# A 192-byte pad ahead of the weight pools, and a larger `plain` count for the first gate-and-up block

## The chip, the cores and the metric

The kernel runs on one core of one Trainium2 chip. The metric is the device time of one execution in microseconds (us). The time before is the median of three runs, 1911.58 us (1909.17 to 1911.75). One further execution was taken with the hardware profiler; it took 1910.38 us, of which 1908.3 us lie between the first and the last instruction (its span).

## The reference

One decoder layer on 256 tokens of width 2048, all in float32. A combined projection feeds three token mixers and their merge gates; then come a SwiGLU feed-forward part and a gated embedding part:

```
h = rms_norm(x, g_mix);  z = h @ w_in            # 2048 x 17424
u_a = short_conv_mixer(...) @ w_sc_out;  u_b = conformer_conv_mixer(...) @ w_cf_out;  u_c = gla_mixer(...) @ w_gla_out
x = x + (sigmoid(m_a)*u_a + sigmoid(m_b)*u_b + sigmoid(m_c)*u_c) @ w_o
gate, up = split(rms_norm(x, g_ffn) @ w_gate_up)  # 2048 x 11264
x = x + (silu(gate) * up) @ w_down
x = x + (p @ w_ple) * sigmoid(rms_norm(x, g_ple) @ w_ple_gate)
return rms_norm(x, g_final)
```

## The kernel before, in words

Every large product is made of matmuls with 128 x 128 of the activations as the stationary operand and 128 x 512 of a weight matrix as the moving operand. A weight tile is loaded as a `raw` tile (128 partitions x 2 x 512 floats, 4096 bytes per partition), and split into two float32r parts: ScalarE writes `whi` (a rounding copy), VectorE writes `wlo = raw - whi`. Activations are split the same way, and each product is the sum of three matmuls: hi by hi, hi by lo, lo by hi. So each 128 x 512 piece of a weight costs six matmuls (three for each half of the 256 tokens), and TensorE (PE) reads its moving operand straight from the `whi` and `wlo` tiles.

The work has two phases, each with its own set of pools (`open_pools`, L481; opened at L489 and L1317). In a pool, a tile's buffers lie one behind the other along a partition, and the pools of a phase are stacked one behind the other.

- **First phase** (L489 to L1316, to about 1069 us of the profile): w_in, the three mixers' output matrices and w_o, in groups of 512 columns. `run` (L655) walks over chunks of four 128-row blocks: it issues the loads two chunks ahead (`issue`, L561, from SyncE's queue), the splits one chunk ahead (`split_w`, L584, which calls `split`, L514), and then the chunk's matmuls (`products`, L639; matmuls at L649 to L651). Its pools are `gla` (one buffer for each of ten tiles), `raws` (5 buffers), `wparts` (5 `whi` and 5 `wlo`), `t4` (5 tiles of 4096 bytes for intermediate results), in this order, and 5 + 3 banks of PSUM. Between the groups stand short batches of other PE work: transposes of results (`transpose_block`, L712), scores of the linear attention (L927, L954), its output (L997 to L999). The stationary operands of the big products (`hhi`, `hlo`, `ohi`, `mT` and others) are tiles of the pool `t8`, which lasts through both phases.
- **Second phase** (from L1317): w_gate_up, w_down, w_ple, w_ple_gate. A recording planner (`Flow`, L114) orders loads, splits, matmuls (`three`, L242; matmuls at L244 to L246) and results by estimated times. Its pools are `raws` (6), `sums` (1), `wparts` (7 and 7), `t4` (3), and 7 + 1 banks of PSUM; the first of them starts at the byte where the first phase's `gla` started.

The pools that last through both phases end at byte 130560 of a partition, which is 255 x 512. The tiles of the first phase's `gla` pool take 4 x 512 + 2048 + 1920 + 1024 + 4096 + 2048 + 1984 = 15168 bytes there (`siga0`, L551, is the last of them), which is 29 x 512 + 320. So `raws`, `wparts` and `t4` of the first phase, whose tiles are all 4096 bytes, begin 320 bytes past a multiple of 512, every buffer of them. In the second phase every such buffer begins at a multiple of 512.

The second phase's gate and up products go in eleven blocks (`Quad`, L63; `add_quad`, L254). A block has eight pairs of 128-row blocks; `PAIRS = "soosooso"` (L1259) gives each pair a kind. Pairs of kind `o` split two raw tiles. Where a pair stands early in its block, at a position below `plain`, both splits are of the usual form. Behind that, the `wlo` of one of the two tiles is made another way (`neg` in `split_ops`, L211 to L225): ScalarE writes `-whi` into it (L220) and a DMA from GpSimd's (POOL's) queue adds the weights from memory onto it (L221), an adding load. Pairs of kind `s` never have an adding load. The two lines that decide it:

```
            kind = g.pairs[p]
...
                               neg=None if pos < g.plain else g.w[:, 2 * p : 2 * p + 2, g.cs[1] : g.cs[1] + NB])
```

`pos` counts the places in `order`. The first block is given an order and a `plain` of its own by `START` (L1426); all other blocks have the order 0 to 7 and `plain` 0.

Of the kernel before, what the change touches and what calls it, by code (L numbers as in the profile page):

```python
# [10 lines left out]
F32 = mybir.dt.float32  # L11
# [8 lines left out]
P = 128  # L20
# [440 lines left out]
def kernel(  # L461
# [17 lines left out]
    pools = {}  # L479

    def open_pools(**sizes):  # L481
# [8 lines left out]
        gla=(1,), raws=(5,), wparts=(5,), t4=(5,), acc=(5, PSUM), misc=(3, PSUM)  # L490
# [58 lines left out]
    s10 = pools["gla"].tile([P, 4, P], F32, name="s10")  # L549
    junk = const.tile([P, NB], F32, name="junk")  # L550
    siga0 = pools["gla"].tile([P, 2, 248], F32, name="siga0")  # L551
    featT = {}

    x_v = x[0].rearrange("(h p) d -> p h d", p=P)
# [781 lines left out]
    def quad_end(j):  # L1336
        def f(g, ps, part):
            v = g.v
            if part == 0:
                g.s = med("gs")  # L1340
            m, s = g.m, g.s

            def sig(h):
                return flow.op("A", 0.7, lambda: act.activation(out=s[:, h, :], in_=m[:, h, :], func=AF.Sigmoid, scale=rr("f", h)))

            def rm(h):
                return flow.op("D", 0.65, lambda: stt(m[:, h, :], m[:, h, :], rr("f", h), s[:, h, :], ALU.mult, ALU.mult))

            def last(h):
                return flow.op("D", 0.65, lambda: stt(m[:, h, :], v[:, h, :], rr("f", h), m[:, h, :], ALU.mult, ALU.mult))  # L1350

            if part == 0:
                return [
                    flow.op("D", 0.7, lambda: tt(m[:, 0, :], m[:, 0, :], ps["2"], ALU.add)),
                    sig(0),
                    rm(0),
                ]
            if part == 1:
                return [
                    flow.op("D", 0.7, lambda: tt(m[:, 1, :], ps["4"], v[:, 1, :], ALU.subtract)),  # L1360
                    sig(1),
                    rm(1),
                ]
            if part == 2:
                return [
                    flow.op("D", 0.7, lambda: tt(v[:, 1, :], v[:, 1, :], ps["5"], ALU.add)),
                    flow.op("D", 0.7, lambda: tt(v[:, 0, :], v[:, 0, :], ps["5"], ALU.add)),
                    last(1),
                ]
            ops = [flow.op("D", 0.7, lambda: tt(v[:, 0, :], v[:, 0, :], ps["3"], ALU.add)), last(0)]  # L1370
            flow.transposes(ops[-1], [a_stat(j, m, z) for z in (0, 2)])
            return ops

        return f
# [13 lines left out]
    def x_part(c, j):  # L1388

        def pe_part(b):  # L1390
            four(b, xr[c], j)

        def rest(b):
            quad_stat(2 * c + j // 2, b, med("sz", (P, 8, P)))

        return pe_part, rest, 2.0, ("f", 2 * c + j // 2)
# [26 lines left out]
        return f  # L1423

    NJ = 11
    START = ((1, 2, 0, 3, 4, 5, 6, 7), 2)  # L1426
    flow.transposes(None, [x_part(3, j) for j in (0, 2)])
    plan = []
    for lo, hi in ((0, 3), (3, 6), (6, 9), (9, NJ)):
        for j in range(lo, hi):  # L1430
            plan.append(Quad(w_gu_v, j * NB, (NJ + j) * NB, PAIRS, quad_mid, quad_end(j), *(START if j == 0 else ())))
        for c in range(4):
# [148 lines left out]
```

## Time and profile before

| | |
|---|---|
| median of three runs | 1911.58 us (1911.75, 1909.17, 1911.58) |
| the profiled execution | 1910.38 us, span 1908.3 us |
| mean granted TensorE clock | 0.996 of full speed |
| busy: PE, VectorE (DVE), ScalarE (ACT), POOL | 98%, 69%, 55%, 4% of the span |
| matmuls | 8589 records |
| adding loads (POOL, L221) | 53 |

How to read it: an engine's busy time is the union of its instructions; matmuls overlap, and their ends are modelled, so the pace of PE is read from the starts of its matmuls. "Idle before" a group is the time its engine stood still just ahead of those instructions, with the engine or transfer that ended the wait. The view by form gives each group of like instructions with its count, busy time and mean duration; the timeline gives single instructions with their start and duration in us. L12 is line 12 of the kernel before; the changed kernel's lines from 552 on have numbers larger by one.

### The profile page before, as it was taken

To read this page: it belongs to the slowest core of one execution; us is meant where nothing else is said; L and a number is where in the kernel's file an instruction comes from. 1 tells how busy PE (TensorE), PEld (TensorE's weight loads), DVE (VectorE), ACT (ScalarE), POOL (GpSimd) and SP (SyncE) were. 2 spreads that over 40 slices of the span, in tenths; PEclk is the share of its full clock that TensorE was granted. 3 is DMA by queue.
4 is the path that set the end of the run, shared out by engine and by line. 5 is a ranking of instruction groups with operands and counts; after the bars stand their busy time and mean duration, and the time that the engine had idled before them with its cause. 6 is when DMAs were issued, how large, how long until landed. Compare 5 with 4: busy or idle time off the path is not lost.

```text
span 1908.3 us, 23192 instructions
## 1 busy us (share of the span) xinstructions
PE 1879.2 (98%) x8589; PEld 1552.6 (81%) x8589; DVE 1320.5 (69%) x1656; ACT 1041.4 (55%) x1205; POOL 72.9 (4%) x75
## 2 busy tenths in 40 slices
PE   8999999999999999999999989999999999999997
PEld 7888888888888888888888778888888888887887
DVE  6457777668888888655556777657866776676654
ACT  6656555554454435644445666546654675465654
POOL 0000000000000000000000011001100110010000
PEclk9999999999999999999999999999999999999999
DMA  8766556556656656676655599769976997698542
GB/s 308 237 180 184 174 174 190 167 154 177 188 179 196 189 160 211 192 234 189 188 185 175 173 254 258 233 197 248 260 240 188 261 253 247 182 259 277 177 163 95
DMA packets 204673, 390.99 MB, mean 205 GB/s; under 512 B 12448, under 2 KB 21280, under 8 KB 204176
## 3 DMA queue, kind: packets, MB, share of 16 engines
q1 hardware_dynamic: 189248, 358.12, 59.0%
q0 software_dynamic: 15312, 31.40, 9.3%
q8 instruction: 67, 1.10, 0.2%
q14 instruction: 46, 0.38, 0.1%
HBM read 387.37 MB, written 2.10 MB: 204 GB/s over the span
## 4 chain that ended last, share of the span: by engine, by line
PE 92%; DMA 4%; DVE 2%; ACT 1%; issue 1%; SPq 0%; DVEq 0%; ACTq 0%
PE acc L651 18%; PE acc L649 18%; PE acc L650 17%; PE acc L245 12%; PE acc L246 12%; PE acc L244 12%; DMA wlo<-in_w_gate_up_dram 2%; DMA raw<-in_w_gate_up_dram 1%; DVE wlo L228 1%; PE tr L718 1%; PE tr L1286 1%; PE sc L927 1%; ACT whi L216 0%; DMA pt<-in_p_feat_dram 0%; DMA x<-in_x_feat_dram 0%
## 5 line engine op out<-in xcount | busy, mean ns | idle before, releaser
L516 DVE TENSOR_TENSOR wlo<-raw,whi 128x1024 fp32r<-128x1024 f32 (+2 forms) x378 | 450.3, 1196 | 302.0 <-ACT whi L515 301.1
L515 ACT ACTIVATE whi<-raw 128x1024 fp32r<-128x1024 f32 (+2 forms) x378 | 390.7, 1036 | 471.9 <-PE acc L651 439.6
L216 ACT ACTIVATE whi<-raw 128x1024 fp32r<-128x1024 f32 (+1 forms) x333 | 332.4, 1006 | 308.4 <-PE acc L246 269.9
L649 PE MATMUL acc<-whi,hhi 128*128 128x512 f32 (+1 forms) x1120 | 436.8, 390 | 5.2 <-ACT whi L515 5.2
L651 PE MATMUL acc<-whi,hlo 128*128 128x512 f32 (+1 forms) x1120 | 433.3, 387 | 0.0
L650 PE MATMUL acc<-wlo,hhi 128*128 128x512 f32 (+1 forms) x1120 | 431.2, 385 | 0.2 <-DVE wlo L516 0.2
L228 DVE TENSOR_TENSOR wlo<-raw,whi 128x1024 fp32r<-128x1024 f32 (+1 forms) x280 | 317.4, 1145 | 155.4 <-ACT whi L216 154.4
L245 PE MATMUL acc<-wlo,st 128*128 128x512 f32 x671 | 262.4, 392 | 7.7 <-DMA wlo<-in_w_gate_up_dram 7.2
L244 PE MATMUL acc<-whi,st 128*128 128x512 f32 x671 | 260.9, 393 | 1.1 <-DVE xr L506 1.0
L246 PE MATMUL acc<-whi,st 128*128 128x512 f32 x671 | 261.6, 391 | 0.0
L649 PEld LDWEIGHTS acc<-whi,hhi 128*128 128x128 f32 x1120 | 211.2, 189 | 46.1 <-ACT whi L515 5.2
L651 PEld LDWEIGHTS acc<-whi,hlo 128*128 128x128 f32 x1120 | 211.0, 188 | 45.0
L650 PEld LDWEIGHTS acc<-wlo,hhi 128*128 128x128 f32 x1120 | 211.1, 189 | 44.5 <-DVE wlo L516 1.1
L245 PEld LDWEIGHTS acc<-wlo,st 128*128 128x128 f32 x671 | 126.5, 189 | 35.7 <-DMA wlo<-in_w_gate_up_dram 9.1
L244 PEld LDWEIGHTS acc<-whi,st 128*128 128x128 f32 x671 | 126.1, 188 | 29.3 <-DVE xr L506 1.4
L246 PEld LDWEIGHTS acc<-whi,st 128*128 128x128 f32 x671 | 126.4, 188 | 26.4
L244 PE MATMUL acc<-whi,aT 128*128 128x512 f32 x352 | 138.3, 393 | 1.3 <-ACT aT L515 1.3
L245 PE MATMUL acc<-wlo,aT 128*128 128x512 f32 x352 | 137.2, 390 | 0.0
L246 PE MATMUL acc<-whi,aT 128*128 128x512 f32 x352 | 136.5, 390 | 0.0
L509 DVE SCALAR_TENSOR_TENSOR cv<-uT,vec,cv 128x255 f32<-128x255 f32 (+15 forms) x240 | 110.9, 467 | 4.8
L221 POOL DMA_DIRECT2D wlo<-in_w_gate_up_dram x53 | 63.8, 1204 | 825.0 <-ACT wlo L220 485.3
L244 PEld LDWEIGHTS acc<-whi,aT 128*128 128x128 f32 x352 | 66.1, 188 | 15.2 <-ACT aT L515 2.0
(276 smaller groups left out, 2078.7 us busy)
## 6 DMA issues: line engine op xcount, KB each, us to landing
raw<-in_w_in_dram SPq DMA_DIRECT2D x262, 512.0 KB, 3.6
raw<-in_w_gate_up_dram SPq DMA_DIRECT2D x176, 512.0 KB, 5.5
raw<-in_w_down_dram SPq DMA_DIRECT2D x88, 512.0 KB, 5.4
wlo<-in_w_gate_up_dram POOLq DMA_DIRECT2D x53, 512.0 KB, 8.6
raw<-in_w_gla_out_dram SPq DMA_DIRECT2D x32, 512.0 KB, 3.7
raw<-in_w_o_dram SPq DMA_DIRECT2D x32, 512.0 KB, 3.8
raw<-in_w_ple_gate_dram SPq DMA_DIRECT2D x24, 512.0 KB, 3.8
raw<-in_w_sc_out_dram SPq DMA_DIRECT2D x16, 512.0 KB, 4.3
```

The costliest lines, as they stand in the source:

```text
L216: a = self._op("A", cost * 0.88, lambda: nc.scalar.activation(out=hi(), in_=src(), func=AF.Copy), deps, load, piece, frees if neg else ())
L221: nc.gpsimd.dma_start(out=lo(), in_=neg, accum_op=ALU.add)
L228: lambda: nc.vector.tensor_tensor(out=lo(), in0=src(), in1=hi().bitcast(F32), op=ALU.subtract),
L244: pe.matmul(o, lhsT=s[0], rhs=w[0], start=start, stop=False)
L245: pe.matmul(o, lhsT=s[0], rhs=w[1], start=False, stop=False)
L246: pe.matmul(o, lhsT=s[1], rhs=w[0], start=False, stop=stop)
L509: dve.scalar_tensor_tensor(out=o, in0=a, scalar=s, in1=b, op0=op0, op1=op1)
L515: a = act.activation(out=hi, in_=src, func=AF.Copy)
L516: b = dve.tensor_tensor(out=lo, in0=src, in1=hi.bitcast(F32), op=ALU.subtract)
L649: pe.matmul(o, lhsT=shi[:, hs], rhs=whi, start=st, stop=False)
L650: pe.matmul(o, lhsT=shi[:, hs], rhs=wlo, start=False, stop=False)
L651: pe.matmul(o, lhsT=slo[:, hs], rhs=whi, start=False, stop=sp)
```

## The change

```diff
@@ -549,6 +549,7 @@
     s10 = pools["gla"].tile([P, 4, P], F32, name="s10")
     junk = const.tile([P, NB], F32, name="junk")
     siga0 = pools["gla"].tile([P, 2, 248], F32, name="siga0")
+    pools["gla"].tile([P, 48], F32, name="pad")
     featT = {}
@@ -1423,7 +1424,7 @@
     NJ = 11
-    START = ((1, 2, 0, 3, 4, 5, 6, 7), 2)
+    START = ((1, 2, 0, 3, 4, 5, 6, 7), 4)
     flow.transposes(None, [x_part(3, j) for j in (0, 2)])
```

The first part adds a tile of 48 floats, 192 bytes per partition, that nothing writes or reads. The `gla` pool becomes 15360 bytes, 30 x 512, and all buffers of `raws`, `wparts` and `t4` of the first phase move up by 192 bytes, to a multiple of 512. Nothing of the second phase moves. PSUM doesn't either.

The second part lets the first block's pairs at positions 0 to 3 do without an adding load, where before it was positions 0 and 1. In its order (1, 2, 0, 3, 4, ...) the kinds are o, o, s, s, o, o, s, o: positions 2 and 3 are pairs of kind `s`, which have none in any case.

No engine's instructions change in kind, number, order or waits; only addresses and the numbers in names do. ScalarE's rows around the first block's first two adding loads, as they stood before (`whi` and `wlo` are the parts, `raw` the loaded weights; L220 is the copy with the sign changed, which stands ahead of each adding load):

```order
L216 ACTIVATE whi_8499<-raw_8364 128x1024
L216 ACTIVATE whi_8512<-raw_8377 128x1024
L220 ACTIVATE wlo_8500<-whi_8499 128x1024
L216 ACTIVATE whi_8521<-raw_8434 128x1024
L216 ACTIVATE whi_8537<-raw_8449 128x1024
L220 ACTIVATE wlo_8522<-whi_8521 128x1024
```

And in the changed kernel:

```order
L216 ACTIVATE whi_8500<-raw_8365 128x1024
L216 ACTIVATE whi_8513<-raw_8378 128x1024
L220 ACTIVATE wlo_8501<-whi_8500 128x1024
L216 ACTIVATE whi_8522<-raw_8435 128x1024
L216 ACTIVATE whi_8538<-raw_8450 128x1024
L220 ACTIVATE wlo_8523<-whi_8522 128x1024
```

Nothing moved: the numbers in the names are larger by one, for the pad, and both adding loads of the pairs at positions 4 and 5 are there as before.

## The prediction

> **What bounds the kernel now.** I read the page first, then PE's waits in each phase, then the starts of single matmuls in the timeline.
>
> ```profile
> span 1908.3 us, 23192 instructions
> PE 1879.2 (98%) x8589; PEld 1552.6 (81%) x8589; DVE 1320.5 (69%) x1656; ACT 1041.4 (55%) x1205; POOL 72.9 (4%) x75
> ```
>
> PE is busy for 98% of the span. A change helps only if it takes time out of PE's own stream or out of one of its few waits. In the first phase (0 to 1069 us) the view of waits gives PE these alone (engine, line, what it waited for, us in total, times, longest):
>
> ```profile
> PE acc L649 <- ACT whi L515: 5.2, 1, 5.2
> PE mu L1095 <- DVE rw L1093: 1.7, 1, 1.7
> PE acc L650 <- DVE wlo L516: 0.2, 1, 0.2
> ```
>
> 5.2 us are the start of the kernel, 1.7 us the mean of the layer norm; together 7.1 us of 1069. So there the time is the number of matmuls times the pace at which PE takes them. Durations don't show that pace, since ends are modelled; starts do. First and last of the 177 matmuls that the timeline of PE gives for 560 to 600 us, in the first phase, with nothing else between them:
>
> ```profile
> 559.67 0.39 PE L651 MATMUL acc<-whi,hlo 128*128 128x512 f32 x1
> ...
> 599.95 0.39 PE L650 MATMUL acc<-wlo,hhi 128*128 128x512 f32 x1
> ```
>
> That is (599.95 - 559.67) / 176 = 0.2289 us from start to start. The same for the 178 matmuls of 1226 to 1266 us in the second phase, of the same shape, with the same three products in the same order:
>
> ```profile
> 1225.84 0.39 PE L244 MATMUL acc<-whi,aT 128*128 128x512 f32 x1
> ...
> 1265.96 0.39 PE L244 MATMUL acc<-whi,aT 128*128 128x512 f32 x1
> ```
>
> (1265.96 - 1225.84) / 177 = 0.2267 us. The first phase is slower by 2.2 ns a matmul, 1%, with PE never waiting in either stretch. What differs is the pools: in the first phase `whi` and `wlo` start 320 bytes past a multiple of 512, in the second at a multiple.
>
> **The pad, part by part.** *PE's pace.* I take the second phase's pace as what aligned moving tiles give. How many matmuls it touches, from the view by form:
>
> ```profile
> L649 PE MATMUL acc<-whi,hhi 128*128 128x512 f32 x1056 | 418.5, 397 | 5.2 <-ACT whi L515 5.2
> L649 PE MATMUL acc<-whi,mT 128*128 128x512 f32 x128 | 50.6, 395 | 0.0
> L649 PE MATMUL acc<-whi,ohi 128*128 128x512 f32 x128 | 50.4, 394 | 0.0
> L649 PE MATMUL acc<-whi,cfhi 128*128 128x512 f32 x64 | 25.1, 392 | 0.0
> L649 PE MATMUL acc<-whi,schi 128*128 128x512 f32 x64 | 25.0, 390 | 0.0
> L649 PE MATMUL acc<-whi,hhi 128*128 128x264 f32 x64 | 18.3, 286 | 0.0
> ```
>
> The 512-wide rows sum to 1440, and L650 and L651 have as many each: 4320 matmuls. At 2.2 ns that is 9.5 us.
>
> *What the breaks take back.* Aligned matmuls don't go at full pace at once. After four transposes in the second phase:
>
> ```profile
> 1220.59 0.60 PE L1286 MATMUL tr<-ident,ga 128*128 128x128 f32 x4
> 1220.94 0.48 PE L244 MATMUL acc<-whi,aT 128*128 128x512 f32 x1
> 1221.26 0.40 PE L245 MATMUL acc<-wlo,aT 128*128 128x512 f32 x1
> ...
> 1223.80 0.39 PE L244 MATMUL acc<-whi,aT 128*128 128x512 f32 x1
> ```
>
> From 1221.26 to 1223.80 there are 11 steps of 0.231 us, no better than the first phase's pace now. So behind each break 11 matmuls gain nothing. How many breaks the phase has, by the view by form:
>
> ```profile
> L718 PE MATMUL tr<-ident,sgb 128*128 128x128 f32 x32 | 4.1, 272 | 0.0
> L927 PE MATMUL sc<-XQ,XK 128*128 128x128 f32 x112 | 13.7, 275 | 0.0
> ```
>
> About 45: 21 batches of eight transposes (the `sgb` row holds four of them), seven batches of 16 scores (112 / 16), and, by the program, some 17 of other kinds. 45 x 11 = 495, and (4320 - 495) x 2.2 ns = 8.4 us.
>
> *A stretch that is slower still.* From the break for the layer norm's mean to the one for its variance, 72 matmuls run in a second steady pace:
>
> ```profile
> 732.52 0.40 PE L649 MATMUL acc<-whi,schi 128*128 128x512 f32 x1
> ...
> 749.09 0.40 PE L651 MATMUL acc<-whi,hlo 128*128 128x512 f32 x1
> ```
>
> (749.09 - 732.52) / 71 = 0.2334 us, 4.5 ns more than the rest of the phase. If aligned tiles end that too, 72 x 4.5 ns = 0.3 us more.
>
> *The 264-wide matmuls* (3 x 64 = 192): the trace has none with aligned tiles. I bound them by the 512-wide difference either way, 192 x 2.2 ns = 0.4 us, and take 0.
>
> *DVE, ACT and the loads.* The same operation in both phases, unaligned first:
>
> ```profile
> L515 ACT ACTIVATE whi<-raw 128x1024 fp32r<-128x1024 f32 x358 | 377.9, 1058 | 450.4 <-PE acc L651 421.4 <-issue 14.2 <-DVE cv L509 6.7
> L216 ACT ACTIVATE whi<-raw 128x1024 fp32r<-128x1024 f32 x292 | 306.8, 1058 | 270.2 <-PE acc L246 236.7 <-issue 18.7 <-DVE xr L506 12.2
> L516 DVE TENSOR_TENSOR wlo<-raw,whi 128x1024 fp32r<-128x1024 f32 x358 | 436.2, 1223 | 286.5 <-ACT whi L515 285.7
> L228 DVE TENSOR_TENSOR wlo<-raw,whi 128x1024 fp32r<-128x1024 f32 x239 | 289.2, 1223 | 146.0 <-ACT whi L216 145.0
> raw<-in_w_in_dram SPq DMA_DIRECT2D x262, 512.0 KB, 3.6
> raw<-in_w_ple_gate_dram SPq DMA_DIRECT2D x24, 512.0 KB, 3.8
> ```
>
> 1058 and 1058 ns, 1223 and 1223 ns: alignment is nothing to either engine. A load lands in 3.6 us unaligned and 3.8 us aligned. All of it lies behind PE, so 0. These rows also say what hides it: in the first phase ACT and DVE stand idle for 450.4 and 286.5 us ahead of their splits, waiting for PE's buffers, directly or through ACT. A PE that is 1% faster leaves them that cover. DVE is fullest in the convolution stretch (columns: us, then PE, PEld, DVE, ACT, POOL busy):
>
> ```profile
> 480.00:720.00 240.00, 240.00 (x1068) 197.51 (x1067) 206.55 (x333) 103.67 (x108) 0.00 (x0) 1.00 0.60 183
> ```
>
> 206.55 of 240 us; at the new pace the stretch is 237.7 us, so DVE still fits. What is late next there is the 1.7 us wait for the mean, a fixed chain on DVE that stays.
>
> *A rule weighed against these rows.* The Trainium skill, page "TensorE: Matmul & The Clock Gate", section "Wait — 56ns, not 53.3ns?", has the start-to-start time of warm matmuls as N / 2.4 GHz plus about 2.5 ns: 215.7 ns at N = 512, a function of N alone. By that rule the two phases would go at one pace, and the pad would be worth 0. The trace differs: 228.9 and 226.7 ns, both over it and apart from each other.
>
> **The other edit.** `plain` 4 in place of 2 reaches positions 2 and 3, and these are pairs of kind `s`. The instructions of all engines stand as before, the 53 adding loads included. So it is worth 0 with certainty. What it would have been worth had it reached position 4: the first adding load, and PE's wait for it.
>
> ```profile
> 1093.00 1.24 POOL L221 DMA_DIRECT2D wlo<-in_w_gate_up_dram  x1 [246.68 <-DVE wlo L228]
> 1103.56 0.79 PE L245 MATMUL acc<-wlo,st 128*128 128x512 f32 x1 [6.85 <-DMA wlo<-in_w_gate_up_dram]
> ```
>
> That wait of 6.85 us stays. All of the second phase starts earlier by what the first one gains, and its addresses don't change.
>
> **The sum.** 8.4 + 0.3 + 0 = 8.7 us off the profiled execution's 1910.38 us, 1901.7 us. The profiled execution is 1.2 us under the median; off the median of 1911.58 us it is 1902.9 us, faster by 0.46%. A measurement of this kernel can tell about 0.2% (3.8 us) from no change.
>
> **The rivals.**
>
> *No change (1911.6 us).* The pace of the first phase hangs on something else that ends with it. For it: the two phases also differ in PSUM (5 + 3 banks in turn against 7 + 1), and each set of pools is seen once. 320 bytes are no odd address either. Against it: PSUM tiles start at whole banks in both phases, stationary tiles come from the same pool, and the slow pace holds through five kinds of stationary operand. By the Trainium skill, page "SBUF — State Buffer", section "Door 1: The DMA port swizzle", lines of SBUF are 16 bytes; 320 is 20 of them, and by that rule this rival would be right. No run here shows what 320 bytes do by themselves.
>
> *Half of it (1907.2 us).* The first phase has two steady paces, 0.2289 and 0.2334 us, so a pace is something that PE locks into at a break. If aligned tiles lock into 0.2267 us after half of the breaks only, the gain is 8.7 / 2 = 4.4 us. Against it: in the second phase PE comes back to 0.2267 us behind its breaks, as in the rows above.
>
> *Slower (1930 us).* The matmuls of the attention's output have an aligned moving tile (`vp`, of the pool `t8`), and a stationary one (`sp`, of `t4`) that starts at 320 bytes:
>
> ```profile
> 385.29 0.39 PE L997 MATMUL ov<-vp,sp 128*128 128x512 f32 x1
> ...
> 387.15 0.40 PE L999 MATMUL ov<-vp,sp 128*128 128x512 f32 x1
> ```
>
> Nine of them, (387.15 - 385.29) / 8 = 0.2325 us: alignment of the moving tile alone doesn't bring the fast pace, and they run near 0.2334 us. If the pad locks the whole first phase at that pace, it costs (4320 - 72) x 4.5 ns = 19 us. It decides from the point where over a third of the phase, 8.7 / (8.7 + 19), locks there and not at 0.2267 us. Against it: behind the change both operands are aligned, as in the second phase, which doesn't show that pace as a steady one.
>
> **How the numbers follow.** The step of 2.2 ns stands exactly where the addresses change, on identical work, so the forecast has 0.78, half 0.06, no change 0.12, slower 0.04. The range: at its low end nothing is lost at the breaks and the 264-wide matmuls gain too, 9.5 + 0.3 + 0.4 = 10.2 us, off a run that is 2.4 us under the median, as one of the three was: 1899.0 us. At its high end it takes in the half, 1907.2, with a little scatter: 1908.0 us. That leaves out no change and slower, 0.16, and little of the rest. Faster by over 0.2% (under 1907.8 us) is the forecast and most of the half, 0.83; within 0.2% is no change and the rest, 0.13; slower 0.04.
>
> **What would show it.** In the profile of the changed kernel, 177 matmuls between 560 and 600 us should become 178, 0.2267 us from start to start, and the stretch behind the mean should have no 0.2334 us. PE's waits in the first phase should stay near 7.1 us, L515 at 1058 ns and L516 at 1223 ns. The second phase should start near 1060 in place of 1069 us and last as long as before, with 53 adding loads and PE's wait of some 7 us for the first of them. I am wrong if the pace stays at 0.2289 us, if it goes to 0.2334 us, or if PE's waits grow by what the pace gives.

## The result, and the profile after

The changed kernel takes 1900.88 us (median of five runs, 1899.80 to 1905.06), the kernel before 1911.58 us (five runs, 1909.17 to 1912.52): ratio 0.9948, 95% interval 0.9937 to 0.9959, so 0.4 to 0.6% faster. The forecast was 1902.9 us. The profiled execution of the changed kernel took 1900.55 us, 9.8 us less than that of before. All its line numbers from 552 on are larger by one.

The head of its page, to be held against that of before:

```profile
span 1898.4 us, 23192 instructions
PE 1870.0 (99%) x8589; PEld 1552.6 (82%) x8589; DVE 1318.7 (69%) x1656; ACT 1041.7 (55%) x1205; POOL 73.0 (4%) x75
```

Same instructions, same counts; PE is busy 9.2 us less. The matmuls that the timeline of PE gives for 560 to 600 us of the changed kernel (start, duration, line, output and inputs), first and last of 178:

```profile
559.75 0.39 PE L652 MATMUL acc<-whi,hlo 128*128 128x512 f32 x1
...
599.87 0.39 PE L652 MATMUL acc<-whi,hlo 128*128 128x512 f32 x1
```

(599.87 - 559.75) / 177 = 0.2267 us from start to start, where it was 0.2289. The 72 matmuls behind the layer norm's mean:

```profile
726.26 0.39 PE L650 MATMUL acc<-whi,schi 128*128 128x512 f32 x1
...
742.36 0.39 PE L652 MATMUL acc<-whi,hlo 128*128 128x512 f32 x1
```

(742.36 - 726.26) / 71 = 0.2268 us, where it was 0.2334. PE's waits in the first phase (engine, line, what it waited for, us in total, times, longest):

```profile
PE acc L650 <- ACT whi L515: 5.1, 1, 5.1
PE mu L1096 <- DVE rw L1094: 1.7, 1, 1.7
PE acc L651 <- DVE wlo L516: 0.5, 1, 0.5
```

7.3 us in all, against 7.1: no new wait took the place of the gain. Where the phases meet, the last big matmul and the first transposes, changed kernel and then the kernel before:

```profile
1059.40 0.39 PE L652 MATMUL acc<-whi,mT 128*128 128x512 f32 x1
1059.89 0.33 PE L1287 MATMUL tr<-ident,xr 128*128 128x128 f32 x1
```

```profile
1068.83 0.40 PE L651 MATMUL acc<-whi,mT 128*128 128x512 f32 x1
1069.32 0.33 PE L1286 MATMUL tr<-ident,xr 128*128 128x128 f32 x1
```

The first phase ends 1069.32 - 1059.89 = 9.43 us earlier. The second takes 1898.4 - 1059.89 = 838.5 us, before 1908.3 - 1069.32 = 839.0 us: the same within what two executions differ by. So nearly all of the 9.8 us lies in the first phase, and in the pace. The other engines' rows by form:

```profile
L515 ACT ACTIVATE whi<-raw 128x1024 fp32r<-128x1024 f32 x358 | 378.3, 1059 | 442.9 <-PE acc L652 375.2 <-DVE cv L509 39.8 <-issue 15.4
L516 DVE TENSOR_TENSOR wlo<-raw,whi 128x1024 fp32r<-128x1024 f32 x358 | 436.0, 1223 | 277.8 <-ACT whi L515 277.1
raw<-in_w_in_dram SPq DMA_DIRECT2D x262, 512.0 KB, 3.6
```

1059 and 1223 ns and 3.6 us, against 1058, 1223 and 3.6 with the same tiles at 320: the start changes nothing here for ScalarE, VectorE or the loads. The idle time of ScalarE and VectorE ahead of their splits shrank from 450.4 to 442.9 us and from 286.5 to 277.8 us, as a PE that is done sooner leaves less of it. Of the second edit, the adding loads and PE's wait for the first of them:

```profile
L221 POOL DMA_DIRECT2D wlo<-in_w_gate_up_dram x53 | 63.8, 1204 | 823.6 <-ACT wlo L220 489.6 <-DVE wlo L228 244.8 <-PE acc L246 89.2
...
1093.97 0.79 PE L245 MATMUL acc<-wlo,st 128*128 128x512 f32 x1 [6.71 <-DMA wlo<-in_w_gate_up_dram]
```

53 still, and 6.71 us where it was 6.85: `plain` 4 does nothing.

### The profile page after: what moved, and what is told of

The parts are those of the page before. It is cut to its first block, busy times and chain, and to the rows that moved or that the text cites. A ratio compares the mean times of both kernels' runs of the same rounds, so it can differ in the third digit from the quotient of the medians.

```text
span 1898.4 us, 23192 instructions
## 1 busy us (share of the span) xinstructions
PE 1870.0 (99%) x8589; PEld 1552.6 (82%) x8589; DVE 1318.7 (69%) x1656; ACT 1041.7 (55%) x1205; POOL 73.0 (4%) x75
## 4 chain that ended last, share of the span: by engine, by line
PE 92%; DMA 4%; DVE 3%; ACT 1%; issue 1%; SPq 0%; DVEq 0%; ACTq 0%; POOLq 0%
PE acc L652 17%; PE acc L651 17%; PE acc L650 17%; PE acc L245 12%; PE acc L246 12%; PE acc L244 12%; DMA wlo<-in_w_gate_up_dram 2%; DMA raw<-in_w_gate_up_dram 1%; DVE wlo L228 1%; PE tr L719 1%; PE tr L1287 1%; PE sc L928 1%; ACT whi L216 0%; DMA x<-in_x_feat_dram 0%; DMA pt<-in_p_feat_dram 0%
```

## The experiments

The forecast rested on an address that differs between the phases, and left three things open: is it the parts' own start or something that moved with it, is it a multiple of 512 that counts, and what do other starts cost? Twelve kernels follow. Each edit is against the changed kernel. The expectations name their theories by letters; where one came up only after a miss, it is said in the words around it. "Start" below is the start of an operand in bytes past a multiple of 512: "moving" that of `whi` and `wlo`, "stationary" that of the pool `t8`, which is 0 where nothing else is said. All paces are from starts in the timeline of PE at 560 to 600 us, first and last matmul quoted, and with their count. The kernel before, run beside these, had medians of 1911.3, 1910.9 and 1911.0 us on the three occasions.

**pad64: the pad at 16 floats.** Moving at 384.

```diff
-    pools["gla"].tile([P, 48], F32, name="pad")
+    pools["gla"].tile([P, 16], F32, name="pad")
```

> The pad of the changed kernel cut from 192 to 64 bytes: the first phase's raws, wparts and t4 start at 384 past a multiple of 512, a multiple of 128 but not of 256. Theory A (what counts is 128 bytes): matmuls of the first phase 0.2267 us from start to start, time near 1901 us. Theory B (512 bytes, as the change says) or C (256 bytes): 0.2289 us or slower, near 1911 us.

Measured: 1925.86 us (one run), 15 us more than before. Its 174 matmuls, and the largest of PE's waits in its first phase:

```profile
559.67 0.39 PE L650 MATMUL acc<-whi,hhi 128*128 128x512 f32 x1
...
599.88 0.39 PE L652 MATMUL acc<-whi,hlo 128*128 128x512 f32 x1
```

```profile
PE acc L650 <- ACT whi L515: 5.2, 1, 5.2
```

(599.88 - 559.67) / 173 = 0.2324 us, with the same wait at the start. B and C had it slower than A, but near 1911 us; no theory had it that far out. Here a start at a multiple of 128 is worse than one at 320. The time follows the pace: 4320 x (0.2324 - 0.2267) = 25 us over the changed kernel, and 1925.86 - 1900.88 = 25.0.

**pad448: the pad at 112 floats.** Moving at 256.

```diff
-    pools["gla"].tile([P, 48], F32, name="pad")
+    pools["gla"].tile([P, 112], F32, name="pad")
```

> The pad enlarged to 448 bytes: the first phase's buffers start at 256 past a multiple of 512. Theories A (128 bytes) and C (256 bytes): 0.2267 us from start to start, near 1901 us. Theory B (512 bytes): 0.2289 us, near 1911 us.

Measured: 1900.97 us (one run). Its 178 matmuls:

```profile
559.79 0.39 PE L651 MATMUL acc<-wlo,ohi 128*128 128x512 f32 x1
...
599.91 0.39 PE L651 MATMUL acc<-wlo,hhi 128*128 128x512 f32 x1
```

0.2267 us: a start at 256 does as well as one at a multiple of 512.

**parts_aligned: only `whi` and `wlo` at 0.** `raws` and `t4` go back to 320.

```diff
-        gla=(1,), raws=(5,), wparts=(5,), t4=(5,), acc=(5, PSUM), misc=(3, PSUM)
+        gla=(1,), raws=(5,), pada=(1,), wparts=(5,), padb=(1,), t4=(5,), acc=(5, PSUM), misc=(3, PSUM)
...
-    pools["gla"].tile([P, 48], F32, name="pad")
+    pools["pada"].tile([P, 48], F32, name="pada")
+    pools["padb"].tile([P, 80], F32, name="padb")
```

> Only the split parts whi and wlo of the first phase are aligned to 512 bytes; raw tiles and t4 tiles start at 320 as before the change. My theory (PE reads its moving operand faster from an aligned start): 0.2267 us, ratio to before near 0.995. Rival (what counts is the writing of raws or intermediate results at odd offsets, in the way of PE's reads): 0.2289 us, ratio 1.000.

Measured: 1902.72 us (four runs, 1902.15 to 1903.53), ratio to before 0.9954 (0.9939 to 0.9968). Its 178 matmuls:

```profile
559.71 0.39 PE L652 MATMUL acc<-wlo,hhi 128*128 128x512 f32 x1
...
599.83 0.39 PE L652 MATMUL acc<-wlo,hhi 128*128 128x512 f32 x1
```

0.2267 us, and a ratio whose interval holds that of the change: the weight parts alone carry it.

**parts_off: all but `whi` and `wlo` at 0.** The reverse, with the pad kept.

```diff
+    pools["pada"].tile([P, 80], F32, name="pada")
+    pools["padb"].tile([P, 48], F32, name="padb")
```

(and the same two pools in `open_pools`.)

> The mirror: raws and t4 aligned, whi and wlo at 320. My theory: 0.2289 us from start to start in the first phase, ratio to before 1.000. Rival (raws or intermediate results): 0.2267 us, ratio 0.995.

Measured: 1911.27 us (ten runs, 1909.39 to 1913.11), ratio to before 0.9998 (0.9989 to 1.0008). Its 176 matmuls:

```profile
559.77 0.39 PE L653 MATMUL acc<-wlo,hhi 128*128 128x512 f32 x1
...
599.82 0.39 PE L654 MATMUL acc<-whi,hlo 128*128 128x512 f32 x1
```

(599.82 - 559.77) / 175 = 0.2289 us, the pace of before, and its time. With parts_aligned this settles which tiles matter: where `raws` and `t4` lie is worth nothing that these times show.

**ph2_off: the second phase's parts at 320.** The first phase stays as changed.

```diff
-    phase = open_pools(raws=(6,), sums=(1,), wparts=(7,), t4=(3,), acc=(1, PSUM), misc=(1, PSUM))
+    phase = open_pools(pad2=(1,), raws=(6,), sums=(1,), wparts=(7,), t4=(3,), acc=(1, PSUM), misc=(1, PSUM))
+    pools["pad2"].tile([P, 80], F32, name="pad2")
```

> The changed kernel with the second phase's pools moved up by 320 bytes, t8 left aligned. If the pace follows the address and not the phase: second phase 0.2289 us in place of 0.2267, some 3400 matmuls x 2.2 ns = 7.5 us back, less at the many breaks, so 1906 to 1909 us, ratio to before 0.997 to 0.999. If it is something else of the second phase: 0.2267 us stays, ratio 0.995.

Measured: 1906.20 us (median of eight runs, 1904.44 to 1908.88), ratio to before 0.9974 (0.9964 to 0.9983). A ninth run, of 3841.59 us, is left out; with it the median is 1906.70. 176 matmuls of its second phase:

```profile
1217.73 0.39 PE L245 MATMUL acc<-wlo,aT 128*128 128x512 f32 x1
...
1257.79 0.39 PE L246 MATMUL acc<-whi,aT 128*128 128x512 f32 x1
```

(1257.79 - 1217.73) / 175 = 0.2289 us. Here the second phase, with its own PSUM banks, planner and code, gets the first phase's old pace from the first phase's old start. That rules out that the pace hung on something else that ends with the first phase. By the view by form, the gate-up and down products have 671 and 352 matmuls on each of three lines, (671 + 352) x 3 = 3069, and 3069 x 2.2 ns = 6.8 us. The medians differ from the changed kernel's by 5.3 us, the spans of the profiled executions by 1905.5 - 1898.4 = 7.1.

**t8_off: the stationary tiles at 320.** Moving stays at 0 in the first phase and goes to 320 in the second.

```diff
+    padt = ctx.enter_context(tc.tile_pool(name="padt", bufs=1))
+    padt.tile([P, 80], F32, name="padt")
...
-    pools["gla"].tile([P, 48], F32, name="pad")
+    pools["gla"].tile([P, 96], F32, name="pad")
```

> The pool t8, from which the stationary operands come, moved up by 320 bytes; the first phase's moving tiles stay at a multiple of 512, and the second phase's moving tiles move to 320 with it. Theory that the moving start alone counts: first phase 0.2267 us from start to start, second phase 0.2289 us. Rival from the output rows of the attention (aligned moving, stationary at 320, 0.2325 us): the stationary start counts too, and the first phase goes at 0.2289 to 0.2334 us.

Measured: 1930.63 us (one run). The 173 matmuls of the first phase, and 178 of the second:

```profile
559.72 0.39 PE L652 MATMUL acc<-whi,hhi 128*128 128x512 f32 x1
...
599.85 0.39 PE L653 MATMUL acc<-wlo,hhi 128*128 128x512 f32 x1
...
1245.70 0.39 PE L244 MATMUL acc<-whi,aT 128*128 128x512 f32 x1
...
1285.82 0.39 PE L244 MATMUL acc<-whi,aT 128*128 128x512 f32 x1
```

(599.85 - 559.72) / 172 = 0.2333 us with the weights aligned, and (1285.82 - 1245.70) / 177 = 0.2267 us with both operands at 320. Both halves missed. So it isn't the moving operand's own start that counts: my theory fell as I had put it. What fits all runs so far is the distance, the moving operand's start less the stationary one's, modulo 256: at 0 the pace is full (theory D). The next four kernels test that.

**both_off: both operands at 320, in both phases.** Nothing is aligned.

```diff
+    padt = ctx.enter_context(tc.tile_pool(name="padt", bufs=1))
+    padt.tile([P, 80], F32, name="padt")
```

> The pool t8 (stationary operands) and all weight and intermediate pools of both phases start at 320 past a multiple of 512: nothing is aligned, and moving and stationary operands stand at the same offset. Theory D (what counts is the distance between the moving and the stationary start, by 256 bytes): 0.2267 us from start to start in both phases, time 1901 us, ratio to before 0.9945. Rival (each operand has to be aligned by itself): 0.2289 to 0.2334 us, 1911 to 1930 us.

Measured: 1901.64 us (four runs, 1901.00 to 1903.17), ratio to before 0.9952 (0.9935 to 0.9968). Its 178 matmuls:

```profile
559.82 0.39 PE L652 MATMUL acc<-whi,ohi 128*128 128x512 f32 x1
...
599.94 0.39 PE L652 MATMUL acc<-whi,hhi 128*128 128x512 f32 x1
```

0.2267 us. All of the gain is there with no operand at a multiple of 512, of 256 or of 128: what counts isn't where either operand starts, but where one starts against the other.

**pad128: the pad at 32 floats.** Moving at 448, distance 192, the one that t8_off's first phase had as 0 less 320.

```diff
-    pools["gla"].tile([P, 48], F32, name="pad")
+    pools["gla"].tile([P, 32], F32, name="pad")
```

> The pad is 128 bytes: the first phase's moving tiles start at 448, that is 192 past a multiple of 256, the stationary ones at 0. By theory D this distance is the one that the first phase had with the stationary pool moved to 320 and the moving tiles at 0: 0.2334 us from start to start, near 1930 us. If each operand's own address counts, no forecast follows, and a pace between 0.2267 and 0.2289 us is as likely.

Measured: 1928.88 us (one run). Its 173 matmuls:

```profile
559.75 0.39 PE L652 MATMUL acc<-whi,hlo 128*128 128x512 f32 x1
...
599.89 0.39 PE L650 MATMUL acc<-whi,hhi 128*128 128x512 f32 x1
```

(599.89 - 559.75) / 172 = 0.2334 us. Two different pairs of starts with the same distance give the same pace, as theory D had it.

**pad224: the pad at 56 floats.** Moving at 32.

```diff
-    pools["gla"].tile([P, 48], F32, name="pad")
+    pools["gla"].tile([P, 56], F32, name="pad")
```

> The pad is 224 bytes: the first phase's moving tiles start 32 past a multiple of 512. If the step is 64 bytes (offsets below it cost nothing): 0.2267 us, 1901 us. If any distance other than a multiple of 256 costs: between 0.2267 and 0.2289 us, 1901 to 1911 us; half of the cost at 64 bytes would be 1906 us.

Measured: 1931.92 us (one run), a miss for both. Its 173 matmuls:

```profile
559.77 0.40 PE L651 MATMUL acc<-wlo,hhi 128*128 128x512 f32 x1
...
599.90 0.40 PE L652 MATMUL acc<-whi,hlo 128*128 128x512 f32 x1
```

(599.90 - 559.77) / 172 = 0.2333 us: 32 bytes of distance cost more than 64. The pace isn't a smooth function of the distance.

**wlo_off: `wlo` alone at 320.** It gets a pool of its own; `raw`, `whi` and `t4` stay at 0.

```diff
-        gla=(1,), raws=(5,), wparts=(5,), t4=(5,), acc=(5, PSUM), misc=(3, PSUM)
+        gla=(1,), raws=(5,), wparts=(5,), padw=(1,), wlos=(5,), padb=(1,), t4=(5,), acc=(5, PSUM), misc=(3, PSUM)
...
+    pools["padw"].tile([P, 80], F32, name="padw")
+    pools["padb"].tile([P, 48], F32, name="padb")
...
-                lo = pools["wparts"].tile([P, 2, c.g.n], F32R, tag="wlo", name=nm("wlo"))
+                lo = pools["wlos"].tile([P, 2, c.g.n], F32R, tag="wlo", name=nm("wlo"))
```

> The changed kernel with the wlo tiles alone at 320 in the first phase, whi aligned. Of three matmuls one reads wlo. If each matmul pays for its own moving tile: a third of the loss, 0.2274 us, near 1904 us. If one tile at a distance is enough to put PE out of step for all three: 0.2289 us, near 1911 us.

Measured: 1923.10 us (one run), a miss for both. Its 174 matmuls:

```profile
559.64 0.40 PE L652 MATMUL acc<-whi,hhi 128*128 128x512 f32 x1
...
599.79 0.40 PE L654 MATMUL acc<-whi,hlo 128*128 128x512 f32 x1
```

(599.79 - 559.64) / 173 = 0.2321 us. One matmul in three at distance 64 costs more than all of them there (0.2289). So the price isn't a sum over single matmuls; it depends on the stream that they stand in.

**plain5 and plain6: the first block without its first, or its first two, adding loads.** What the second edit would have been worth, had it reached them: 52 and 51 adding loads in place of 53.

```diff
-    START = ((1, 2, 0, 3, 4, 5, 6, 7), 4)
+    START = ((1, 2, 0, 3, 4, 5, 6, 7), 5)
```

(plain6 has 6 there.)

> The changed kernel with plain 5 in the first block, so that the pair at position 4 really has no adding load: 52 adding loads. PE's wait of some 7 us for the first adding load goes; the next one, at position 5, is late instead by less. I expect 3 to 7 us off the changed kernel, 1894 to 1898 us, ratio to before 0.991 to 0.993. Rival (VectorE, which takes the split over, or the loads are late at the same place): 1900 us, ratio 0.9945.

> Plain 6: positions 4 and 5 without adding loads, 51 in all. If adding loads early in the block are what is late: 1893 to 1897 us, as plain 5 or a little better. If VectorE is the limit in the first block, its two more splits of 1.2 us each cost what the loads gave: no better than plain 5.

Measured: plain5 1898.47 us (five runs, 1896.78 to 1902.63), ratio to before 0.9934 (0.9921 to 0.9946); plain6 1897.26 us (five runs, 1895.00 to 1900.48), 0.9929 (0.9916 to 0.9943). PE's waits for adding loads in the second phase (total, times, longest): the changed kernel, plain5, plain6.

```profile
PE acc L245 <- DMA wlo<-in_w_gate_up_dram: 7.3, 3, 6.7
```

```profile
PE acc L245 <- DMA wlo<-in_w_gate_up_dram: 5.4, 4, 4.0
```

```profile
PE acc L245 <- DMA wlo<-in_w_gate_up_dram: 3.6, 2, 3.2
```

With the first adding load gone the next one is late: of 6.7 us only 1.9 come back (7.3 - 5.4), and 3.7 with both gone. The medians fall by 2.4 and 3.6 us, both a little less than I had expected. VectorE isn't the limit there, since plain6 is no worse than plain5. Both kernels beat the one before by more than the change does, but their intervals overlap that of the change, so they aren't surely told apart from it, nor from each other. plain6 is the best by its median.

## Why the prediction was right, and where its reason was not

- **The bound.** Right: the first phase is PE's matmuls times their pace. In all twelve kernels PE's waits in the first phase came to between 7.1 and 8.5 us, against 7.1 before, and the time went with the pace: pad64 is 25 us over the changed kernel.
- **Which tiles, and that the two phases differ for it.** Right: parts_aligned and parts_off put it on `whi` and `wlo` alone, and ph2_off carries the old pace into the second phase. "No change" falls with that. "Half of it" falls with the changed kernel's timeline: behind every break its long stretches come to 0.2266 or 0.2267 us. The Trainium skill, page "SBUF — State Buffer", section "Door 1: The DMA port swizzle", has lines of 16 bytes. A start 20 whole lines off cost PE 2.2 ns a matmul here, so whole lines alone don't tell PE's pace.
- **"Aligned moving tiles give" the pace.** The step that was wrong, though the number it gave was right. Alignment as such gives nothing (both_off has none, t8_off's first phase has it). The stationary tiles happen to start at a multiple of 512, so to align the moving ones is to bring the distance to 0. That a pad sized for the one gave the other was luck. The Trainium skill's rule that I weighed against the rows (page "TensorE: Matmul & The Clock Gate", section "Wait — 56ns, not 53.3ns?"), a pace that hangs on N alone, fails on the runs either way: at one N, they have five paces from 226.7 to 233.4 ns.
- **"Slower (1930 us)".** Its evidence was real. `ov` reads its moving tile at 0 and its stationary one at 320, distance 192. The prediction's 0.2325 us is from starts given to 0.01 us, over eight steps; to the nanosecond, as the trace has them, these steps are 0.2334 us. That is the pace that the whole first phase has at distance 192 in pad128 and t8_off (0.2333 to 0.2334 us), which took 1929 and 1931 us. I could have read it as a distance: it had a moving operand that was aligned and slow. With the pad at 48 floats that distance doesn't arise in the 512-wide products, and 0.04 was fair. 8.7 / (8.7 + 19) is 0.31, a little under the third that the prediction wrote.
- **"What the breaks take back".** The mis-sized term. I took 45 breaks with 11 matmuls each that gain nothing, 495 x 2.2 ns = 1.1 us. The timeline has 38 stretches of 512-wide matmuls behind breaks, if other widths count as breaks and stretches too short for 11 such steps are left out. Of these, 17 begin as I had it, at 0.230 us a step or a little more; eight go at full pace at once, and the other 13 lie between, at 0.2275 to 0.2289 us. One that goes at full pace and one of the 17, in the changed kernel, behind the eight transposes of `fq` and behind the seven of `G`:

```profile
93.21 1.04 PE L719 MATMUL tr<-ident,fq 128*128 128x128 f32 x8
94.00 0.48 PE L650 MATMUL acc<-whi,hhi 128*128 128x512 f32 x1
94.32 0.39 PE L651 MATMUL acc<-wlo,hhi 128*128 128x512 f32 x1
...
96.82 0.39 PE L650 MATMUL acc<-whi,hhi 128*128 128x512 f32 x1
...
435.78 0.93 PE L719 MATMUL tr<-ident,G 128*128 128x128 f32 x7
436.46 0.47 PE L650 MATMUL acc<-whi,hhi 128*128 128x512 f32 x1
436.77 0.39 PE L651 MATMUL acc<-wlo,hhi 128*128 128x512 f32 x1
...
439.08 0.39 PE L652 MATMUL acc<-whi,hlo 128*128 128x512 f32 x1
```

  (96.82 - 94.32) / 11 = 0.2273 us, and (439.08 - 436.77) / 10 = 0.231. So the breaks take back less. Summed over all 38 from such rows, the first 11 full steps of each stretch got 0.5 us shorter, where I had 0. With 38 breaks the rest is (4320 - 418) x 2.2 ns = 8.6 us; 0.3 us came behind the mean, as forecast, and some 0.2 us from the 36 `ov` matmuls, those of the attention's output. Nine of these in the changed kernel:

```profile
382.24 0.39 PE L998 MATMUL ov<-vp,sp 128*128 128x512 f32 x1
...
384.06 0.39 PE L1000 MATMUL ov<-vp,sp 128*128 128x512 f32 x1
```

  (384.06 - 382.24) / 8 = 0.2275 us, where rows read in the same way gave 0.2325 (to the nanosecond, 0.2266 and 0.2334), and 36 x 6.8 ns = 0.2 us. I had left them out, though `t4`, which holds their stationary tile, moves with the pad. 8.6 + 0.5 + 0.3 + 0.2 = 9.6 us against 9.43 measured; I had 8.7. Two smaller terms are missing from both sums. In the kernel before two more stretches, of 24 matmuls each behind batches of `ov` at 385 and 418 us, went at 0.2334 us, which gave 0.1 us more behind their first 11 steps; and the first 192 matmuls of the program gained 0.1 us where their share was 0.4.
- **ACT, DVE, the loads, `plain` and the second phase at nothing.** Right, by the rows above. The 264-wide matmuls went from 123.0 to 122.8 ns from start to start, on the mean of them all. Only half of them came to distance 0: a tile holds two blocks of 264 floats, 1056 bytes, and so the second starts 32 bytes past a multiple of 256.

## What to carry to other kernels

Where PE is the bound and never waits, read its pace from the starts of its matmuls, stage by stage, and compare stages of the same shape: a step of 1% shows where a busy share shows nothing. Then work out where both operands start: here the pace was full where the moving tile's start less the stationary tile's was a multiple of 256 bytes, so a pad is to be sized on both, and one of the wrong size costs more than the right one brings (15 to 21 us against 10). And a late transfer that is taken away gives back only the time to the next late one: 1.9 of 6.7 us here.

## What was unexpected in the hardware

The pace of the 128 x 512 float32r matmuls by distance (moving less stationary start, modulo 256 bytes), from the stretches quoted above:

| distance | seen in (moving, stationary start modulo 512) | us from start to start |
|---|---|---|
| 0 | the change (0, 0), pad448 (256, 0), both_off and t8_off's second phase (320, 320) | 0.2267 |
| 32 | pad224 (32, 0) | 0.2333 |
| 64 | before, parts_off, ph2_off's second phase (320, 0) | 0.2289 |
| 128 | pad64 (384, 0) | 0.2324 |
| 192 | pad128 (448, 0), t8_off's first phase (0, 320) | 0.2333 to 0.2334 |
| 0 for `whi`, 64 for `wlo` | wlo_off | 0.2321 |

The kernel before sat at the mildest of the bad distances that were tried. That the stationary operand's start has a part in it suggests that its load and the streaming of the moving operand meet somewhere; no run shows where. The Trainium skill, page "TensorE: Matmul & The Clock Gate", section "Step-by-step: what each phase is for", gives PE two independent read ports for the two, so that loading the next weights takes nothing from the running matmul; if they do meet, these runs agree with that only to within 6.7 ns of 226.7.

A pace here is the mean of a pattern. To the nanosecond, the steps of the kernel before go about 226, 229 and 232 ns in turn, all along its stretches at 0.2289 us. Behind most breaks the step of 232 ns begins with the matmul of `whi` and the high part of the activations, behind others with one of the other two. So the cost doesn't belong to one of the three products. Its stretches at 0.2334 us have steps of 233 and 234 ns alone, and in the changed kernel's long stretches all are 226 or 227.

What stays open: where the two meet, why 32 bytes cost more than 64, and why one matmul in three at 64 costs more than all of them. In the big products distance 0 was seen with three pairs of starts and 192 with two, but 32, 64 and 128 with one pair each. At 64 the distance alone doesn't decide. The kernel before held two paces there, 0.2289 us and, in three stretches of 120 matmuls together, 0.2334; the short `ov` batches of t8_off, with the same two starts (320, 0), go at 0.2314 to 0.2334 us. So which pattern PE falls into seems to depend on what it did at the break; that was not tried.
